# Loads of the side work of a hybrid trunk: three queues instead of one, two steps ahead, in finer steps

## The chip, the cores and the metric

The kernel runs on one core of a Trainium2 chip. The core has a matrix engine (TensorE, PE in the profile), a vector engine (VectorE, DVE), an activation engine (ScalarE, ACT), a general engine (GpSimd, POOL) and a synchronisation engine (SyncE, SP). Each takes its instructions in program order. SP, ACT and POOL can also issue transfers (DMAs) between the chip's main memory and the on-chip memory. The metric is the device time of one execution in microseconds (us), lower is better.

## The reference

One layer over 1024 tokens of width 1024, in float32. Four branches read one projection of the normalised input; their outputs are mapped back, merged by gates, projected, and a gated MLP with a short convolution follows. What matters here are three of the branches:

```python
# gMLP: v is normalised over 512 columns, then mixed over the 128 tokens of a block, per head
v = rms_norm(v, v_norm)
w = jnp.where(mask[None], w_s, 0)
sv = jnp.einsum('hts,bnshc->bnthc', w, v) + b_s.T[None, None, :, :, None]
return u * sv.reshape(bsz, seq, GMLP_WIDTH)

# RG-LRU: gates from small per-head products, then a scan over the tokens
r = sigmoid(einsum('bshi,hij->bshj', uh, w_a) + b_a)
log_a = -LRU_C * r * softplus(-lam)
h = scan(h * a + x_in) ; return h * gelu(y)

# gated linear attention (GLA), in chunks of 64 tokens
log_a = log_sigmoid(g_lr @ w_g2 + b_g) / GLA_TAU      # decays, summed up inside a chunk
# scaled queries and keys, then products inside chunks and a state across them
```

## The kernel before, in words

Every large product is made of three products of split operands: a tile is cast (ACT, line 122) and the rest is subtracted (DVE, line 123). On-chip tiles of 128 x 1024 come from one pool of 30 pages; raw weights have two buffers (`wr`).

The program runs in stages (times are those of the profiled execution):

- **gmlp**, 0 to 61 us: for each of 8 tiles of 128 tokens a norm (`hn`), a transpose and split (`hh` by ACT, `hl` by DVE), and the product for v. The normalised v (`vg`) is stored to main memory as `vgd`. The two `sm` instructions on POOL (lines 284 and 285) make a reciprocal root of a norm: one couple for `vg`, one for `hn`.
- **ranks**, to 117 us, then **columns**, 117 to 624 us: 24 *pairs* of column blocks. A pair is seven groups of 12 matmuls (`seven`, line 167), some 19 us of TensorE. Between the groups `work(s)` is called with s = 0 to 5. It applies the pair before's activation (`act`, ACT line 472), stores it (`fm<-za`, `fm<-zb`, POOL line 473), and from pair 4 on takes one step of the side work (`tick`).
- The **side work** is three generators that run one after another: `lru` (four heads), `spatial` (the gMLP mixing, four heads) and `factors` (the GLA's decays, queries and keys, for p = 0 and 1). A step ends at a `yield`. There are 95 ticks and 71 steps. Their inputs are pages in main memory that earlier pairs stored; `fetched_page` loads one, by POOL.
- **gla**, 624 to 718 us: an output gate (PE line 277), then `within` (lines 718 and 720) and `across` for each p and token tile. It reads six pages (`gl`) for each p, and four of `vd`.
- **mixing** and **latent** stages, attention, the merge and the MLP, to 1950 us. `load_o` loads a branch's output (`oraw`).

In columns and in the MLP the orders of ACT, DVE and SP are the order of the code (`manual_schedule`). Elsewhere, and always for PE and POOL, a scheduler orders the instructions when the kernel is built.

```python
def tick(self, n=1):
    for _ in range(n):
        while self.bg:
            try:
                next(self.bg[0])
                break
            except StopIteration:
                self.bg.popleft()
```

Of the kernel before, what the change touches and what calls it, by code (L numbers as in the profile page):

```python
# [17 lines left out]
P = 128  # L18
# [59 lines left out]
class Trunk:  # L78
# [262 lines left out]
    def gmlp(self):  # L341
# [41 lines left out]
        for i in range(NT):  # L383
            if i == 1:
                self.tc.no_sync_barrier()
            if i + 3 < NT:
                load(i + 3)
            if i + 2 < NT:
                norm(i + 2)
            if i == 6:  # L390
                wd = [self.pweights(a["wd"][0], 8, 264, 3)]
            v = self.page("vg")
            for n in range(2):
                ps = self.psum1()
                self.tm(ps[:, 0:256], self.hrows(i), wv[n])
                nc.scalar.activation(out=v[:, n * 256:(n + 1) * 256], in_=ps[:, 0:256], func=AF.Gelu_apprx_tanh)
                if n == 0 and i + 1 < NT:
                    next(step[i + 1], None)
            ss = self.small(1)
            nc.scalar.activation(out=v[:, 512:1024], in_=v[:, 0:512], func=AF.Square, accum_out=ss)  # L400
            r = self.rsqrt(ss, 512, 1)
            nc.vector.scalar_tensor_tensor(out=v[:, 0:512], in0=v[:, 0:512], scalar=r, in1=gv[:, 0:512], op0=ALU.mult, op1=ALU.mult)
            nc.gpsimd.dma_start(out=self.vgd[:, i * 512:(i + 1) * 512], in_=v[:, 0:512])
        wd.append(self.weights(a["wd"][1], 8, 264, 3))
# [54 lines left out]
    def columns(self, first):  # L459
# [28 lines left out]
        def work(s, prev, end):  # L488
# [25 lines left out]

    def fetched_page(self, src, name):
        t = self.page(name)
        self.nc.gpsimd.dma_start(out=t, in_=src)
        return t

    def spatial(self):  # L520
# [4 lines left out]
        w3 = ws[:, 0:512].rearrange("p (h t) -> p h t", h=4)  # L525
        vgd = self.vgd.rearrange("p (i c) -> p i c", i=NT)
        yield
        nc.vector.memset(w3[64:128, :, 0:64], 0.0)
        for h in range(4):
            v, u = self.page("vh"), self.fetched_page(self.fmo[h], "ug")  # L530
            v3 = v.rearrange("p (i c) -> p i c", i=NT)
            for i in (0, 4):
                nc.gpsimd.dma_start(out=v3[:, i:i + 4, :], in_=vgd[:, i:i + 4, h * P:(h + 1) * P])
            yield
# [10 lines left out]
    def lru(self):  # L545
# [20 lines left out]
        nc.vector.tensor_scalar(out=sm8, in0=sp4, scalar1=-2.0, scalar2=None, op0=ALU.mult)  # L566
        lraw = self.fetched_page(a["lw"], "lraw")
        yield
# [4 lines left out]
        for h in range(4):  # L573
            u = self.fetched_page(self.fmo[8 + h], "u")
# [7 lines left out]
            t, x = self.page("t"), self.page("xi")  # L582
            nc.scalar.activation(out=t, in_=ps, func=AF.Sigmoid, bias=prm[:, C_LBA + h:C_LBA + h + 1])
            ps = self.psum()
            self.fm(ps, [lw[4 + h]], [(uh, ul)])
            yield
            nc.scalar.activation(out=x, in_=ps, func=AF.Sigmoid, bias=prm[:, C_LBI + h:C_LBI + h + 1])
            u = self.fetched_page(self.fmo[8 + h], "u")
# [3 lines left out]
            nc.scalar.activation(out=t, in_=t, func=AF.Tanh, scale=sp4[:, h:h + 1])  # L592
            yield
            nc.scalar.activation(out=t, in_=t, func=AF.Sqrt)
            nc.vector.tensor_mul(out=x, in0=x, in1=u)
            yield
            nc.vector.scalar_tensor_tensor(out=x, in0=q, scalar=1.0, in1=x, op0=ALU.add, op1=ALU.mult)
            nc.vector.tensor_mul(out=x, in0=x, in1=t)
            y = self.fetched_page(self.fmo[4 + h], "yg")
            yield  # L600
            nc.vector.tensor_tensor_scan(out=t, data0=q, data1=x, initial=0.0, op0=ALU.mult, op1=ALU.add)
            yield
            nc.vector.tensor_mul(out=t, in0=t, in1=y)
            nc.gpsimd.dma_start(out=self.spill[1][h], in_=t)

    def factors(self):
# [5 lines left out]
        gd = self.page("gd")  # L612
        nc.gpsimd.dma_start(out=gd[:, 0:128], in_=self.gds[:, 0:128])
# [10 lines left out]
        nc.scalar.copy(out=gdt[0:16, :], in_=ps[0:16, :])  # L624
        yield
        for p in range(2):
            ps = self.psum()
# [3 lines left out]

            x, b = self.page("gx"), self.page("gb")
# [4 lines left out]
            nc.scalar.activation(out=b, in_=b, func=AF.Exp, scale=-1.0)  # L637
            nc.scalar.activation(out=b, in_=b, func=AF.Ln, bias=self.one)
            yield
            nc.vector.scalar_tensor_tensor(out=x, in0=x, scalar=0.0, in1=b, op0=ALU.min, op1=ALU.subtract)  # L640
            nc.gpsimd.dma_start(out=self.logs[p], in_=x)
            yield
        for p in range(2):
            x, b, keep = self.fetched_page(self.logs[p], "gx"), self.page("gb"), self.page("keep")
            nc.gpsimd.memset(keep, 1.0)
            nc.gpsimd.memset(c3(keep)[:, :, 0:1], 0.0)
            yield

            nc.vector.tensor_tensor_scan(out=b, data0=keep, data1=x, initial=0.0, op0=ALU.mult, op1=ALU.add)
            yield  # L650
            last, e2 = c3(b)[:, :, 63:64], self.page("e2")
            nc.vector.tensor_sub(out=c3(x), in0=last.to_broadcast([P, 16, 64]), in1=c3(b))
            nc.scalar.activation(out=dec[p].unsqueeze(2), in_=last, func=AF.Exp, scale=1.0 / 16)
            nc.scalar.activation(out=e2, in_=b, func=AF.Exp, scale=-1.0 / 16)
            k = self.fetched_page(self.fmo[14 + p], "qk")
            yield
            dv = dec[p].rearrange("p (b c) -> p b c", c=2)
            nc.vector.tensor_mul(out=self.dec2[p].unsqueeze(2), in0=dv[:, :, 0:1], in1=dv[:, :, 1:2])
            nc.scalar.activation(out=b, in_=b, func=AF.Exp, scale=1.0 / 16)
            nc.scalar.activation(out=x, in_=x, func=AF.Exp, scale=1.0 / 16)  # L660
            yield
            nc.vector.tensor_mul(out=e2, in0=e2, in1=k)
            nc.gpsimd.dma_start(out=self.glo[p][1], in_=e2)
            nc.vector.tensor_mul(out=x, in0=x, in1=k)
            nc.gpsimd.dma_start(out=self.glo[p][2], in_=x)
            q = self.fetched_page(self.fmo[12 + p], "qk")
# [13 lines left out]
            yield  # L680
            ps = self.psum()
            for i in range(NT):
                nc.tensor.transpose(ps[:, i * P:(i + 1) * P], ks2[:, i * P:(i + 1) * P], self.ident)
# [4 lines left out]
            kt = self.page("kt")  # L688
            nc.scalar.copy(out=kt, in_=ps)
            nc.gpsimd.dma_start(out=self.glo[p][5], in_=kt)  # L690

    def gla(self):
# [1000 lines left out]
```

## Time and profile before

| | us |
|---|---|
| median of 3 runs (1953.83 to 1956.97) | 1955.28 |
| the profiled execution, its own time | 1952.54 |
| its span, first to last instruction | 1950.8 |
| around the span (1952.54 - 1950.8) | 1.74 |
| TensorE busy | 1888.8 |
| VectorE, ScalarE, GpSimd busy | 1255.3, 866.9, 238.3 |

The granted clock of TensorE is 0.990 of its full speed over the span. The time is a median of a few executions and the profile is one of them.

### The profile page before, as it was taken

To read this page: it belongs to the slowest core of one execution; us is meant where nothing else is said; L and a number is where in the kernel's file an instruction comes from. 1 tells how busy PE (TensorE), PEld (TensorE's weight loads), DVE (VectorE), ACT (ScalarE), POOL (GpSimd) and SP (SyncE) were. 2 spreads that over 40 slices of the span, in tenths; PEclk is the share of its full clock that TensorE was granted. 3 is DMA by queue.
4 is the path that set the end of the run, shared out by engine and by line. 5 is a ranking of instruction groups with operands and counts; after the bars stand their busy time and mean duration, and the time that the engine had idled before them with its cause. 6 is when DMAs were issued, how large, how long until landed. Compare 5 with 4: busy or idle time off the path is not lost.

```text
span 1950.8 us, 25124 instructions
## 1 busy us (share of the span) xinstructions
PE 1888.8 (97%) x9768; PEld 1609.0 (82%) x9768; DVE 1255.3 (64%) x1752; ACT 866.9 (44%) x1329; POOL 238.3 (12%) x426
## 2 busy tenths in 40 slices
PE   7999999899999899999999999999999999999998
PEld 7988877678788898898788789978888888888887
DVE  4757667555754375717788972587777777774552
ACT  5433565436443132142677734355444444443331
POOL 2100100121202021011122300200000000000101
PEclk9999999899999899999999999999999999999999
DMA  6023344444635317316001343223233232686651
GB/s 241 24 87 130 130 162 161 168 159 153 235 137 195 143 66 267 101 57 220 30 23 32 138 160 132 97 86 108 107 109 117 106 120 101 207 318 214 256 192 44
DMA packets 84439, 269.75 MB, mean 138 GB/s; under 512 B 9584, under 2 KB 11264, under 8 KB 84320
## 3 DMA queue, kind: packets, MB, share of 16 engines
q1 hardware_dynamic: 53712, 157.90, 24.1%
q0 software_dynamic: 30464, 109.98, 14.8%
q8 instruction: 77, 1.26, 0.3%
q14 instruction: 42, 0.34, 0.1%
q10 hardware_dynamic: 144, 0.26, 0.0%
HBM read 187.30 MB, written 80.81 MB: 137 GB/s over the span
## 4 chain that ended last, share of the span: by engine, by line
PE 74%; issue 12%; DVE 6%; POOL 3%; ACT 3%; DMA 2%; POOLq 0%; SPq 0%; DVEq 0%; ACTq 0%
PE bk L167 22%; PE bk L1482 12%; PE ps L268 8%; PE ps L167 8%; PE p L277 8%; PE p L167 3%; PE ps L277 3%; PE ps L1024 2%; PE po L1075 2%; PE p L1209 2%; PE pp L1060 1%; POOL sm L285 1%; DMA oraw<-spill 1%; DVE wl L123 1%; POOL fm L473 1%
## 5 line engine op out<-in xcount | busy, mean ns | idle before, releaser
L122 ACT CAST wh<-t 128x1024 fp32r<-128x1024 f32 x85 | 89.5, 1053 | 295.2 <-PE bk L167 123.2
L167 PE MATMUL bk<-q,wh 128*128 128x512 f32 x704 | 217.0, 389 | 0.5 <-DVE q L123 0.5
L1482 PE MATMUL bk<-dh,g 128*128 128x512 f32 x704 | 217.0, 389 | 0.2 <-DVE q L1493 0.2
L123 DVE TENSOR_TENSOR wl<-wr,wh 128x1024 fp32r<-128x1024 f32 (+7 forms) x110 | 107.3, 977 | 128.4 <-ACT wh L122 127.5
L167 PE MATMUL ps<-S,wh 128*128 128x512 f32 x560 | 175.6, 394 | 3.6 <-ACT zb L216 3.6
L167 PEld LDWEIGHTS bk<-q,wh 128*128 128x128 f32 x704 | 132.1, 188 | 28.1 <-DVE q L123 0.8
L1482 PEld LDWEIGHTS bk<-dh,g 128*128 128x128 f32 x704 | 132.1, 188 | 28.0 <-DVE q L1493 0.6
L122 ACT CAST wh<-wr 128x1024 fp32r<-128x1024 f32 (+7 forms) x110 | 93.5, 852 | 130.9 <-PE ps L268 69.7
L268 PE MATMUL ps<-o,wh 128*128 128x512 f32 x512 | 140.6, 395 | 4.9 <-ACT o L122 2.8
L1482 PE MATMUL bk<-dl,g 128*128 128x512 f32 x352 | 136.9, 389 | 0.0
L167 PE MATMUL bk<-q,wl 128*128 128x512 f32 x352 | 136.9, 389 | 0.0
L167 PEld LDWEIGHTS ps<-S,wh 128*128 128x128 f32 x560 | 105.6, 190 | 27.3 <-ACT zb L216 5.3
L123 DVE TENSOR_TENSOR wl<-t,wh 128x1024 fp32r<-128x1024 f32 x85 | 103.8, 1222 | 34.2 <-ACT wh L122 34.1
L268 PEld LDWEIGHTS ps<-o,wh 128*128 128x128 f32 x512 | 95.5, 189 | 26.9 <-ACT o L122 3.7
L167 PE MATMUL ps<-S,wl 128*128 128x512 f32 x280 | 109.9, 393 | 0.0
L277 PE MATMUL p<-wl,hh 128*128 128x336 f32 (+2 forms) x320 | 94.8, 297 | 0.6 <-DVE wl L123 0.6
L277 PE MATMUL p<-wh,hh 128*128 128x336 f32 (+2 forms) x320 | 94.9, 298 | 0.0
L277 PE MATMUL p<-wh,hl 128*128 128x336 f32 (+2 forms) x320 | 94.8, 297 | 0.0
L167 PE MATMUL bk<-S,wh 128*128 128x512 f32 x304 | 93.5, 389 | 0.0
L123 DVE TENSOR_TENSOR dl<-dr,dh 128x1024 fp32r<-128x1024 f32 x44 | 53.8, 1222 | 43.4 <-ACT dh L122 36.4
L268 PE MATMUL ps<-o,wl 128*128 128x512 f32 x256 | 79.7, 392 | 0.8 <-DVE wl L123 0.8
L167 PEld LDWEIGHTS bk<-q,wl 128*128 128x128 f32 x352 | 66.1, 188 | 13.8
(447 smaller groups left out, 4617.3 us busy)
## 6 DMA issues: line engine op xcount, KB each, us to landing
wr<-in_wf SPq DMA_DIRECT2D x48, 512.0 KB, 4.3
wr<-in_up SPq DMA_DIRECT2D x44, 512.0 KB, 3.8
dr<-in_down SPq DMA_DIRECT2D x44, 512.0 KB, 5.3
g<-fm SPq DMA_DIRECT2D x32, 512.0 KB, 6.0
fm<-za POOLq DMA_DIRECT2D x22, 512.0 KB, 2.9
fm<-zb POOLq DMA_DIRECT2D x22, 512.0 KB, 2.9
gb<-fy POOLq DMA_DIRECT2D x22, 512.0 KB, 2.9
ga<-fy POOLq DMA_DIRECT2D x22, 512.0 KB, 2.9
```

Source lines behind the costliest of these rows:

```text
L122: self.nc.scalar.copy(out=hi, in_=src)
L123: self.nc.vector.tensor_sub(out=lo, in0=src, in1=hi.bitcast(F32))
L167: self.nc.tensor.matmul(ps, l[:, c], r, start=first and k == 0 and j == 0, stop=last and k == 3 and j == 2, skip_group_check=True)
L268: self.nc.tensor.matmul(ps[:, h * 512:(h + 1) * 512], lhs, rhs[:, h * 512:(h + 1) * 512], start=first and k == 0 and j == 0, stop=last and ...
L277: self.nc.tensor.matmul(ps, lhs, rhs, start=first and k == 0 and j == 0, stop=last and k == K - 1 and j == 2)
L285: nc.gpsimd.tensor_tensor(out=r, in0=t, in1=self.mhalf[:, 0:w], op=ALU.pow)
L473: nc.gpsimd.dma_start(out=self.fmo[idx], in_=z)
L1024: nc.tensor.matmul(ps[:, off + c0:off + c1], l[:, q0], r[:, c0:c1], start=jj == 0, stop=jj == 2)
L1060: nc.tensor.transpose(pp[:, at:at + P], probs[u][j][0][:, kb * P:(kb + 1) * P], self.ident)
L1075: nc.tensor.matmul(po[:, c], vs[2 * m + kk][:, head * P:(head + 1) * P], ptt[:, z * 512 + kk * 256:z * 512 + kk * 256 + c.stop - c.start], ...
L1209: self.nc.tensor.matmul(ps, l, x, start=k == 0 and j == 0, stop=k == K - 1 and j == 2)
L1482: nc.tensor.matmul(ps, l, r[:, halves[c]], start=first and n == 0 and j == 0, stop=last and n == len(gs) - 1 and j == 2)
```

## The change

1. gmlp's eight stores of `vg` to `vgd` are issued by SP instead of POOL.
2. `fetched_page` issues by SP unless it is given a queue; the side work gives it ACT's. So the loads of `lru`, `spatial` and `factors` (27 of them) are ACT's, and the GLA's pages, `vd` and the `oraw` loads are SP's.
3. The side work has finer steps: `lru` 40 instead of 35, `spatial` 10 instead of 9, `factors` 33 instead of 27. Loads stand about two steps ahead of their use. `spatial` loads head h + 1 while it works on head h, and a `vh` page comes by one DMA instead of two halves.
4. `factors` keeps the first decay page (p = 0) on chip; only that of p = 1 is stored and loaded again. Exp and Ln are taken for both p in succession.
5. In the last pair, at s = 5, four pages of p = 0 (1, 3, 4, 2) are loaded; `gla` then loads four of p = 1, then the rest.

```diff
-            nc.gpsimd.dma_start(out=self.vgd[:, i * 512:(i + 1) * 512], in_=v[:, 0:512])
+            nc.sync.dma_start(out=self.vgd[:, i * 512:(i + 1) * 512], in_=v[:, 0:512])
...
+            if end and s == 5:
+
+                self.gl = [{j: self.fetched_page(self.glo[0][j], "gl") for j in (1, 3, 4, 2)}, {}]
...
-    def fetched_page(self, src, name):
+    def fetched_page(self, src, name, queue=None):
         t = self.page(name)
-        self.nc.gpsimd.dma_start(out=t, in_=src)
+        (queue or self.nc.sync).dma_start(out=t, in_=src)
         return t
...
+        def fetch(h):
+            v = self.page("vh")
+            nc.scalar.dma_start(out=v.rearrange("p (i c) -> p i c", i=NT), in_=vgd[:, :, h * P:(h + 1) * P])
+            return v, self.fetched_page(self.fmo[h], "ug", nc.scalar)
+
+        nxt = fetch(0)
         yield
         nc.vector.memset(w3[64:128, :, 0:64], 0.0)
+        yield
         for h in range(4):
-            v, u = self.page("vh"), self.fetched_page(self.fmo[h], "ug")
-            v3 = v.rearrange("p (i c) -> p i c", i=NT)
-            for i in (0, 4):
-                nc.gpsimd.dma_start(out=v3[:, i:i + 4, :], in_=vgd[:, i:i + 4, h * P:(h + 1) * P])
+            v, u = nxt
+            if h < 3:
+                nxt = fetch(h + 1)
             yield
...
         for p in range(2):
-            x, b, keep = self.fetched_page(self.logs[p], "gx"), self.page("gb"), self.page("keep")
+            nc.scalar.activation(out=gb[p], in_=gb[p], func=AF.Exp, scale=-1.0)
+        yield
+        for p in range(2):
+            nc.scalar.activation(out=gb[p], in_=gb[p], func=AF.Ln, bias=self.one)
...
+        nc.gpsimd.dma_start(out=self.logs[1], in_=gx[1])
+        yield
+        x = gx[0]
+        for p in range(2):
+            if p:
+                x = self.fetched_page(self.logs[1], "gx", nc.scalar)
+            b, keep = self.page("gb"), self.page("keep")
             nc.gpsimd.memset(keep, 1.0)
             nc.gpsimd.memset(c3(keep)[:, :, 0:1], 0.0)
             yield
+            yield
...
+        for p, js in ((1, (1, 3, 4, 2)), (0, (5, 0)), (1, (5, 0))):
+            self.gl[p].update((j, self.fetched_page(self.glo[p][j], "gl")) for j in js)
         for p in range(2):
-            qs, ki, ks, qb0, qb1, kt = (self.fetched_page(t, "gl") for t in self.glo[p])
+            qs, ki, ks, qb0, qb1, kt = (self.gl[p][j] for j in range(6))
...
         if raw is None:
-            raw = self.page("oraw")
-            self.nc.gpsimd.dma_start(out=raw, in_=self.spill[k][h])
+            raw = self.fetched_page(self.spill[k][h], "oraw")
             yield
```

How the change moves instructions, at three places. Names carry the number of their buffer; `<-` has the target on its left.

**Place one, gmlp.** SP's order early in the program, before (`x` are the inputs of the norm, `wr` raw weights whose casts stand in ACT's order between those of `vg`):

```order
L349 DMA x_253<-in_x 128x1024
L349 DMA x_301<-in_x 128x1024
L349 DMA x_384<-in_x 128x1024
L131 DMA wr_943<-in_wd 128x792
L131 DMA wr_949<-in_wd 128x792
L349 DMA x_466<-in_x 128x1024
L131 DMA wr_955<-in_wd 128x528
```

and of the change:

```order
L349 DMA x_253<-in_x 128x1024
L349 DMA x_301<-in_x 128x1024
L403 DMA vgd<-vg_311 128x512
L349 DMA x_384<-in_x 128x1024
L131 DMA wr_943<-in_wd 128x792
L131 DMA wr_949<-in_wd 128x792
L349 DMA x_466<-in_x 128x1024
```

The first store of `vg` now stands ahead of three loads on SP, and is gone from POOL.

**Place two, the spatial mixing.** POOL's order before, in the pair in which `spatial` begins (`spill` is lru's last result, `fm` the pair's stores, `ws` the mixing weights and their bias, `ug` and `vh` the operands of one head):

```order
L604 DMA spill_3_90<-t_3126 128x1024
L473 DMA fm_121<-za_3089 128x1024
L473 DMA fm_122<-zb_3090 128x1024
L523 DMA ws_3276<-in_wst 128x512
L524 DMA ws_3276<-in_gmlp_b_s 128x512
L517 DMA ug_3300<-fm_99 128x1024
L533 DMA vh_3299<-vgd 128x4x128 x2
L517 DMA ug_3356<-fm_100 128x1024
L533 DMA vh_3355<-vgd 128x4x128 x2
```

and ACT's order of the change at the same place:

```order
L472 ACTIVATE za_3225<-za_3225 128x1024
L206 COPY za_3362<-p_430_3365 128x512
L472 ACTIVATE zb_3226<-zb_3226 128x1024
L533 DMA vh_3404<-vgd 128x8x128
L520 DMA ug_3406<-fm_99 128x1024
L216 COPY zb_3363<-ps_3364 128x512
L533 DMA vh_3442<-vgd 128x8x128
L520 DMA ug_3444<-fm_100 128x1024
L122 CAST wh_3446<-t_436_3408 128x1024
```

The operands of the heads have moved from POOL, behind `ws`, to ACT. The two loads of `ws` stay on POOL behind the same stores, and DVE's MEMSET of `ws`, which waits for the first of them, keeps its place between the pair's subtractions.

**Place three, the GLA's pages.** POOL's order before, at the end of the pairs (`fm_145` and `fm_146` are the last pair's stores; `gl_0_...` names a page's number, 155 to 160 are those of p = 0, 161 to 166 those of p = 1):

```order
L517 DMA gl_4966<-gl_5_160 128x1024
L517 DMA gl_4968<-gl_0_161 128x1024
L517 DMA gl_4970<-gl_1_162 128x1024
L473 DMA fm_145<-za_4825 128x1024
L473 DMA fm_146<-zb_4826 128x1024
L517 DMA gl_4972<-gl_2_163 128x1024
L517 DMA gl_4974<-gl_3_164 128x1024
L517 DMA gl_4976<-gl_4_165 128x1024
L517 DMA gl_4978<-gl_5_166 128x1024
```

and SP's order of the change (`wr<-in_wog` are the gate's weights, four loads of which the first two are issued early in the last pair, the third when a `wr` buffer comes free):

```order
L131 DMA wr_4901<-in_wog 128x1024
L520 DMA gl_4920<-gl_1_156 128x1024
L520 DMA gl_4922<-gl_3_158 128x1024
L520 DMA gl_4924<-gl_4_159 128x1024
L520 DMA gl_4926<-gl_2_157 128x1024
L131 DMA wr_4981<-in_wog 128x1024
L520 DMA gl_4957<-gl_1_162 128x1024
L520 DMA gl_4959<-gl_3_164 128x1024
L520 DMA gl_4961<-gl_4_165 128x1024
L520 DMA gl_4963<-gl_2_163 128x1024
```

The pages of p = 1 that `within` reads (1 to 4) no longer stand behind the last pair's stores; they stand behind the third load of the gate's weights.

## Rows read from the trace of the kernel before

**Rows 1.** The page: busy time, share of the span and instructions of each engine

```profile
PE 1888.8 (97%) x9768; PEld 1609.0 (82%) x9768; DVE 1255.3 (64%) x1752; ACT 866.9 (44%) x1329; POOL 238.3 (12%) x426
```

**Rows 2.** Waits of PE by cause: us in total, times, longest us

```profile
PE ps L537 <- DMA vh<-vgd: 12.0, 4, 7.0
...
PE ps L718 <- DMA gl<-gl: 7.2, 1, 7.2
PE ps L167 <- ACT zb L216: 3.6, 2, 2.9
PE ps L268 <- ACT o L122: 2.8, 2, 2.1
```

**Rows 3.** Stretches: us, busy of PE, PEld, DVE, ACT, POOL; clock, DMA share, GB/s

```profile
380.20:390.40 10.20, 5.02 (x19) 4.56 (x20) 2.70 (x4) 0.00 (x0) 2.07 (x3) 0.50 0.77 257
...
520.00:523.60 3.60, 2.94 (x7) 2.36 (x8) 2.83 (x3) 3.51 (x6) 0.50 (x1) 0.53 0.52 198
...
641.00:647.00 6.00, 5.71 (x29) 5.71 (x30) 1.53 (x5) 0.00 (x0) 0.53 (x1) 0.55 1.02 413
...
25.00:50.00 25.00, 23.65 (x199) 23.25 (x198) 13.52 (x15) 14.06 (x26) 8.29 (x18) 1.00 0.52 181
...
448.00:470.00 22.00, 22.00 (x94) 17.31 (x93) 13.33 (x18) 16.21 (x18) 2.67 (x5) 1.00 0.37 137
```

**Rows 4.** Spatial mixing in order of time: POOL (idle before, its cause)

```profile
373.42 0.56 POOL L523 DMA_DIRECT2D ws<-in_wst  x1
...
377.93 0.78 POOL L533 DMA_DIRECT2D vh<-vgd  x1 [2.80 <-issue]
```

**Rows 5.** The same for PE, DVE and ACT

```profile
383.32 2.04 PE L537 MATMUL ps<-ws,vh 128*128 128x128 f32 x8 [7.01 <-DMA vh<-vgd]
...
378.17 0.27 DVE L528 MEMSET ws<- 64x256 f32 x1 [4.26 <-DMA ws<-in_wst]
...
371.32 1.06 ACT L472 ACTIVATE zb<-zb 128x1024 f32<-128x1024 f32 x1
```

**Rows 6.** Transfers of 370 to 400 us: issues, KB each, median us to landing

```profile
vh<-vgd POOLq DMA_DIRECT2D x4, 256.0 KB, 3.5
...
ws<-in_gmlp_b_s POOLq DMA_DIRECT2D x1, 256.0 KB, 7.3
```

**Rows 7.** DVE in the factors, in order of time

```profile
509.56 2.29 DVE L649 TENSOR_TENSOR_SCAN gb<-keep,gx 128x1024 f32<-128x1024 f32 x1 [5.03 <-DMA gx<-log]
```

**Rows 8.** Around the start of gla in order of time: POOL, SP, PE

```profile
631.94 0.55 POOL L473 DMA_DIRECT2D fm<-za  x1 [9.01 <-ACT za L472]
...
633.49 2.42 POOL L517 DMA_DIRECT2D gl<-gl  x4
...
601.57 21.94 SPq L131 DMA_DIRECT2D wr<-in_wog  x4
...
641.29 1.65 PE L718 MATMUL ps<-gl,gl 128*128 128x128 f32 x6 [7.17 <-DMA gl<-gl]
```

**Rows 9.** The page: transfers of the whole kernel, as in rows 6

```profile
wr<-in_wf SPq DMA_DIRECT2D x48, 512.0 KB, 4.3
...
fm<-za POOLq DMA_DIRECT2D x22, 512.0 KB, 2.9
```

**Rows 10.** ACT at the start of mixing(3), in order of time

```profile
880.59 1.05 ACT L122 CAST o<-oraw 128x1024 fp32r<-128x1024 f32 x1 [3.18 <-DMA oraw<-spill]
```

**Rows 11.** gmlp, in order of time: POOL, ACT, PE

```profile
25.23 0.62 POOL L403 DMA_DIRECT2D vgd<-vg  x1 [1.08 <-DVE gq L943]
...
32.48 0.61 POOL L403 DMA_DIRECT2D vgd<-vg  x1 [1.08 <-DVE vg L402]
...
26.76 1.61 ACT L122 CAST wh<-wr 128x792 fp32r<-128x792 f32 x2
29.76 1.04 ACT L313 ACTIVATE hn<-x 128x1024 f32<-128x1024 f32 x1
...
37.13 0.39 PE L277 MATMUL p<-pwh,hl 128*128 128x256 f32 x1 [1.00 <-DVE hl L123]
```

More of the change, by code (lines that the diff above doesn't have):

```diff
@@ L566, in lru @@
         nc.vector.tensor_scalar(out=sm8, in0=sp4, scalar1=-2.0, scalar2=None, op0=ALU.mult)
-        lraw = self.fetched_page(a["lw"], "lraw")
+        lraw = self.fetched_page(a["lw"], "lraw", nc.scalar)
+        u = self.fetched_page(self.fmo[8], "u", nc.scalar)
+        yield
         yield
@@ L573, in lru @@
         for h in range(4):
-            u = self.fetched_page(self.fmo[8 + h], "u")
             yield
@@ L581, in lru @@
             yield
-            t, x = self.page("t"), self.page("xi")
+            t = self.page("t")
             nc.scalar.activation(out=t, in_=ps, func=AF.Sigmoid, bias=prm[:, C_LBA + h:C_LBA + h + 1])
@@ L585, in lru @@
             self.fm(ps, [lw[4 + h]], [(uh, ul)])
+            u = self.fetched_page(self.fmo[8 + h], "u", nc.scalar)
             yield
+            x = self.page("xi")
             nc.scalar.activation(out=x, in_=ps, func=AF.Sigmoid, bias=prm[:, C_LBI + h:C_LBI + h + 1])
-            u = self.fetched_page(self.fmo[8 + h], "u")
+            yield
             q = self.page("q")
@@ L592, in lru @@
             nc.scalar.activation(out=t, in_=t, func=AF.Tanh, scale=sp4[:, h:h + 1])
+            nc.vector.tensor_mul(out=x, in0=x, in1=u)
             yield
             nc.scalar.activation(out=t, in_=t, func=AF.Sqrt)
-            nc.vector.tensor_mul(out=x, in0=x, in1=u)
+            nc.vector.scalar_tensor_tensor(out=x, in0=q, scalar=1.0, in1=x, op0=ALU.add, op1=ALU.mult)
+            y = self.fetched_page(self.fmo[4 + h], "yg", nc.scalar)
             yield
-            nc.vector.scalar_tensor_tensor(out=x, in0=q, scalar=1.0, in1=x, op0=ALU.add, op1=ALU.mult)
             nc.vector.tensor_mul(out=x, in0=x, in1=t)
-            y = self.fetched_page(self.fmo[4 + h], "yg")
             yield
             nc.vector.tensor_tensor_scan(out=t, data0=q, data1=x, initial=0.0, op0=ALU.mult, op1=ALU.add)
+            if h < 3:
+                u = self.fetched_page(self.fmo[9 + h], "u", nc.scalar)
             yield
@@ L612, in factors @@
         gd = self.page("gd")
-        nc.gpsimd.dma_start(out=gd[:, 0:128], in_=self.gds[:, 0:128])
+        nc.scalar.dma_start(out=gd[:, 0:128], in_=self.gds[:, 0:128])
         w2, gdt = self.page("w2"), self.page("gdt")
@@ L625, in factors @@
         yield
+        gx, gb = [None] * 2, [None] * 2
         for p in range(2):
@@ L630, in factors @@
             yield
-            x, b = self.page("gx"), self.page("gb")
+            x, b = gx[p], gb[p] = self.page("gx"), self.page("gb")
             bg = prm[:, C_GBG + p:C_GBG + p + 1]
@@ L636, in factors @@
             yield
[L637 to L642, printed above, removed]
-        for p in range(2):
-            x, b, keep = self.fetched_page(self.logs[p], "gx"), self.page("gb"), self.page("keep")
+        for p in range(2):
+            nc.scalar.activation(out=gb[p], in_=gb[p], func=AF.Exp, scale=-1.0)
+        yield
+        for p in range(2):
+            nc.scalar.activation(out=gb[p], in_=gb[p], func=AF.Ln, bias=self.one)
+        yield
+        for p in range(2):
+            nc.vector.scalar_tensor_tensor(out=gx[p], in0=gx[p], scalar=0.0, in1=gb[p], op0=ALU.min, op1=ALU.subtract)
+        nc.gpsimd.dma_start(out=self.logs[1], in_=gx[1])
+        yield
+        x = gx[0]
+        for p in range(2):
+            if p:
+                x = self.fetched_page(self.logs[1], "gx", nc.scalar)
+            b, keep = self.page("gb"), self.page("keep")
             nc.gpsimd.memset(keep, 1.0)
@@ L647, in factors @@
             yield
+            yield
             nc.vector.tensor_tensor_scan(out=b, data0=keep, data1=x, initial=0.0, op0=ALU.mult, op1=ALU.add)
+            k = self.fetched_page(self.fmo[14 + p], "qk", nc.scalar)
             yield
@@ L652, in factors @@
             nc.vector.tensor_sub(out=c3(x), in0=last.to_broadcast([P, 16, 64]), in1=c3(b))
+            yield
             nc.scalar.activation(out=dec[p].unsqueeze(2), in_=last, func=AF.Exp, scale=1.0 / 16)
             nc.scalar.activation(out=e2, in_=b, func=AF.Exp, scale=-1.0 / 16)
-            k = self.fetched_page(self.fmo[14 + p], "qk")
             yield
@@ L658, in factors @@
             nc.vector.tensor_mul(out=self.dec2[p].unsqueeze(2), in0=dv[:, :, 0:1], in1=dv[:, :, 1:2])
+            nc.vector.tensor_mul(out=e2, in0=e2, in1=k)
+            nc.scalar.activation(out=x, in_=x, func=AF.Exp, scale=1.0 / 16)
+            nc.gpsimd.dma_start(out=self.glo[p][1], in_=e2)
+            q = self.fetched_page(self.fmo[12 + p], "qk", nc.scalar)
+            yield
             nc.scalar.activation(out=b, in_=b, func=AF.Exp, scale=1.0 / 16)
[L660 to L663, printed above, removed]
             nc.vector.tensor_mul(out=x, in0=x, in1=k)
             nc.gpsimd.dma_start(out=self.glo[p][2], in_=x)
-            q = self.fetched_page(self.fmo[12 + p], "qk")
             yield
@@ L671, in factors @@
             nc.vector.tensor_copy(out=s4[:, :, 1, :], in_=k4[:, :, 1, :])
+            yield
             nc.vector.tensor_mul(out=b, in0=b, in1=q)
             yield
+            ps = self.psum()
+            for i in range(NT):
+                nc.tensor.transpose(ps[:, i * P:(i + 1) * P], ks2[:, i * P:(i + 1) * P], self.ident)
             qb = [self.page("qb") for _ in range(2)]
@@ L680, in factors @@
             yield
-            ps = self.psum()
-            for i in range(NT):
-                nc.tensor.transpose(ps[:, i * P:(i + 1) * P], ks2[:, i * P:(i + 1) * P], self.ident)
+            kt = self.page("kt")
+            nc.scalar.copy(out=kt, in_=ps)
+            nc.gpsimd.dma_start(out=self.glo[p][5], in_=kt)
             q4 = b.rearrange("p (b c t) -> p b c t", c=2, t=64)
@@ L687, in factors @@
             yield
-            kt = self.page("kt")
-            nc.scalar.copy(out=kt, in_=ps)
-            nc.gpsimd.dma_start(out=self.glo[p][5], in_=kt)
     def gla(self):
```

## The prediction

> **What bounds the kernel now.** I read the page first: TensorE is busy for 1888.8 of 1950.8 us [rows 1], so only its 62 us of idleness, and the time in which it runs below full clock, are to be had. The view of its waits says for whom it stood: 12.0 us in four waits for the pages of the spatial mixing, 7.2 in one for the GLA's pages, 3.6 in two for ScalarE's copy `zb` (the longest 2.9), 2.8 in two for the casts of `oraw` [rows 2]. Then I took stretches behind these waits and looked at the granted clock. It stands at 0.50 to 0.55 behind the three long ones, which is the lower of its two levels (1.2 and 2.4 GHz), and at 1.00 in 25 to 50 us, where the engine had stood for only 1.00 us at a time [rows 3, 11]. A long wait therefore costs more than itself. I price the surplus as busy time x (1 - clock): 5.02 x 0.50 = 2.5, 2.94 x 0.47 = 1.4, and 5.71 x 0.45 = 2.6 us [rows 3]. Last, the orders by time show what each wait ends on.
>
> **Spatial mixing.** Before, POOL issues `ws`, then the heads' loads; the first `vh` half is issued at 377.93 after 2.80 of idleness that the profile lays to nothing else, and the product starts at 383.32 after 7.01 of standing [rows 4, 5]. The change issues `vh` by ScalarE behind the activation that ends at 372.4 [rows 5], and the later heads a step or more before their products. So 12.0 + 2.5 = 14.5 us go, less what is late next. Two things can be.
> First `ws`. It stays on POOL at its place, 373.42, and VectorE's MEMSET of it waits until 378.17 and ends at 378.44 [rows 4, 5]. In the change the first spatial product stands four matmuls later in TensorE's order than before (behind all 12 matmuls of the group S3, where it was behind 8). A matmul of the pairs takes 22.00/94 = 0.23 us [rows 3], and TensorE stopped at 383.32 - 7.01 = 376.3, so it comes there at 377.1 or so and stands 1.4 for the MEMSET. VectorE's own later work (three splits and an addition) is due about when TensorE needs it.
> Second the whole `vh` page. No row shows it in one transfer: it is 1024 pieces of 512 bytes where a half had 512. Halves land 3.5 us after issue, and the slowest load there took 7.3 [rows 6]; so the page lands between 375.9 and 379.7, and the wait is 0 to 2.6. Its issue costs ScalarE between 0.56 (POOL's for `ws`) and 3.6 (POOL's 0.78 with the idleness of 2.80 ahead) [rows 4]; I take the low end, for want of a cause of the 2.80 on ScalarE's queue. I take the page as landing no later than `ws` does, and keep 1.4 in all (0 to 4.3, which is the MEMSET's whole delay). Between a stand of 1.0 that left the clock alone and one of 2.9 that cost 1.4, I take half of that, 0.7. **Spatial: 14.5 - 2.1 = 12.4 gained.**
>
> **Factors.** VectorE's scan waits 5.03 for the page that has just been stored [rows 7]; all behind it is late, ScalarE's `zb` copy too, on which TensorE stands 2.9. For p = 0 the load is gone. For p = 1 it comes two steps ahead. **2.9 + 1.4 = 4.3 gained** (down to 0 if another step holds ScalarE there).
>
> **GLA's pages.** POOL holds the last four of the twelve behind the last pair's stores: 9.01 of waiting for ScalarE until 631.94, the pages from 633.49 [rows 8], and TensorE stands 7.2. In the change the four pages of p = 0 are issued after the second of the gate's weights, about 604. Those of p = 1 follow the third, which was issued about 622 when a `wr` buffer came free (the row of the four ends at 601.57 + 21.94 = 623.5) [rows 8]. At full load the DMAs move 413 GB/s [rows 3], so 0.5 MB takes 1.3 us. The weights land at 622 + 4.3 = 626.3 at the latest [rows 9], the four pages by 631.5. TensorE began to wait for p = 1 at 641.29 - 7.17 = 634.1 [rows 8], so 2.6 us are in hand. **7.2 + 2.6 = 9.8 gained.** Nine more loads follow (four `gl`, `vd`, the last weights) and end near 643 by the same 1.3; what reads them stands behind the products that 641 to 647 are full of.
> The stretch 641 to 647 has the DMA share at 1.02 [rows 3], so one may hold that transfers, not the issue, set the time. The Trainium skill (DMA: Bandwidth & Descriptors, section "Issuing engines are not separate DMA queues") says so in general: transfers issued by ScalarE, SyncE and GpSimd run on the same 16 DMA engines, and using several issuers only saves the time to initiate. Read that way, four issues of 2.42 us are the whole gain here, and the sum is 7.4 less. The row of 9.01 speaks against it: the pages waited for an activation, not for a DMA engine.
>
> **oraw.** ScalarE waits 3.18 for a page [rows 10]; of TensorE's 2.8 the shorter wait, 0.7, depends on it. SP isn't held by GpSimd's work. **0.7 gained** (0 to 2.8).
>
> **gmlp.** Here the change loses. The store of the first `vg` follows its data, at 25.23 [rows 11]. On SP the loads `x_384`, `wr_943` and `wr_949`, which waited for nothing of the kind, come behind it. With 0.56 for each issue [rows 4] the last leaves at 25.23 + 3 x 0.56 = 26.9, and lands 4.3 later, at 31.2 [rows 9]. ScalarE casts the second `wr` at 26.76 + 0.80 = 27.6 before [rows 11]; so all behind is 3.6 late, `hn` of the next tile too. But POOL is rid of its store. The square of `hn` ended at 29.76 + 1.04 = 30.8, yet its couple on POOL came behind the second store of `vg`, which waited for VectorE and ended at 32.48 + 0.61 = 33.1 [rows 11]. So 2.3 of the 3.6 come back, and TensorE stands 1.00 + 1.3 = 2.3 instead of 1.00 at 37. I take 1.3 and, as above, 0.7 for the clock: **2.0 lost** (0 to 3.6 + 1.4 = 5.0).
>
> **The rest.** ScalarE issues 27 loads at some 0.56 us: 15 us over 12 pairs, beside work that takes 16.21 of 22.00 even in a busy pair [rows 3], so they hide; without that cover they are 15 us. The finer steps add 12 ticks of the 24 unused ones and nothing to do. The smaller waits of TensorE in the pairs may change either way; I leave them.
>
> **Sum:** 12.4 + 4.3 + 9.8 + 0.7 - 2.0 = 25.2 us off the profiled execution's 1952.54, which gives 1927.3. The median stands 2.74 above that execution, so **1930.1**. About 0.2% (4 us) is what a measurement of this kernel can tell from no change.
>
> **The rivals.**
> *The heads still wait.* The whole `vh` page, or its place on an in-order engine, makes it land late: four products stand as long as the slowest load exceeds a half's, 7.3 - 3.5 = 3.8 for the first, less for the others, 7 to 10 us in all with the clock's share: 1937 to 1940. For it: the page's size and rows 6. Against: three of four loads are over ten microseconds ahead.
> *The transfers are the bound.* Then the stands only shift: the pages' issue of 2.42 and POOL's 2.80 are saved, gmlp's 2.0 lost: 3.2, so 1952. The rule of the Trainium skill cited above would have it so. For it: shares of 0.77 and 1.02. Against: the causes in rows 7 and 8 are late issues.
> *More is gained.* The gmlp store and the MEMSET cost nothing (+4.1), the longer `oraw` wait goes too (+2.1), and some small waits: 1923.
> *Slower.* ScalarE is in order. A load whose page was last read by a store waits for that store's landing, 2.9 us [rows 9], and the copies that empty TensorE's accumulators stand behind it. If each of the 27 loads cost TensorE 1.2, it would be 32 lost: 1930.1 + 32 = 1962. It decides from 25.2/27 = 0.93 a load. For it: TensorE has stood on just these copies. Against: ScalarE has some 6 us free in a pair of 22, and in the order only the last `ug` follows closely on the store it waits for.
>
> **How the numbers follow.** Likeliest 0.60 (its own range 1923 to 1939, by the bounds of `ws`, gmlp and `oraw`), heads late 0.13, more gained 0.10, transfers 0.07, slower 0.10. The range 1920 to 1946 leaves out the last two. Faster by over 0.2%: 0.60 + 0.13 + 0.10 = 0.83; same 0.07; slower 0.10.
>
> **What would show it.** Right: no wait for `vh` over 3 us, no half clock behind the GLA's first products, the first `gl` landing before 616, the scan without its 5 us; a longer wait for `hl` near 40 us; a MEMSET of `ws` still some 4 us late. Wrong: waits on `zb` or `za` copies that end behind a DMA on ScalarE, or TensorE waiting for `gl` behind the third weights.

## The result, and the profile after

The changed kernel takes **1935.53 us** (median of 4, 1934.66 to 1935.97) against 1954.93 beside it: a ratio of 0.9899, 95% interval 0.9882 to 0.9916. Predicted were 1930.1, 1920 to 1946. The profiled execution took 1935.97 with a span of 1934.2, so the spans differ by 16.6; before's profiled execution lay 2.4 below that median and the changed kernel's 0.4 above its own, which is the 2.8 between 16.6 and 19.4. Stages are compared by spans, whole kernels by medians.

TensorE's waits by cause show at once that the change did what it says and paid elsewhere (columns as in rows 2; the view's first line, 8.0 ahead of the first product as in the kernel before, and others are left out):

```profile
...
PE ps L268 <- DVE o L123: 5.9, 1, 5.9
PE ps L547 <- DVE ws L538: 3.6, 1, 3.6
PE p L277 <- ACT hh L122: 2.9, 2, 2.0
PE p L277 <- ACT vg L396: 2.7, 2, 1.9
...
PE p L277 <- DVE hl L123: 2.2, 2, 1.7
...
PE ps L268 <- ACT o L122: 1.8, 2, 1.5
```

The waits for `vh`, for `gl` and for `zb` of [rows 2] are gone. In their place stand one of 5.9 for a split of `oraw`, one of 3.6 for the MEMSET of `ws`, and new ones in gmlp. By stages, from TensorE's first instruction of each, this is the account of 16.6:

| stage | before | after | difference | predicted |
|---|---|---|---|---|
| gmlp and ranks, to the first pair | 116.6 | 121.7 | +5.1 | +2.0 |
| pairs, to the first `within` | 516.4 | 498.5 | -17.9 | -16.7 |
| gla and mixing(0), to the transposes behind it (729.8 before) | 96.7 | 86.8 | -9.9 | -9.8 |
| to the transposes of the latents | 164.3 | 170.1 | +5.8 | -0.7 |
| the rest of the span | 1056.7 | 1057.1 | +0.4 | 0 |

Each column is one profiled execution, and the same code doesn't take the same time in each. In the five traces with `vg`'s stores on SP the first pair begins at 118.3 to 123.4, in the eight with them on POOL at 115.5 to 116.8: the loss in gmlp is real, but lies between 1.5 and 7.9. The pairs of the kernel before took 519.5 in another build with the same code there (516.4 here), those of the changed kernel 498.4 and 500.1 in two others (498.5 here).

**The pairs.** Stretches of that stage (columns as in rows 3), first of the kernel before:

```profile
116.60:633.10 516.50, 497.96 (x2211) 405.41 (x2210) 317.11 (x406) 244.62 (x286) 72.24 (x127) 0.99 0.44 157
```

and of the changed kernel, with the stretch behind its stand at `ws`, one of gla, and the start of mixing(3):

```profile
121.70:620.20 498.50, 492.71 (x2211) 404.11 (x2210) 316.28 (x406) 242.18 (x283) 48.58 (x86) 1.00 0.45 161
402.00:406.00 4.00, 3.92 (x19) 3.74 (x20) 3.56 (x4) 0.00 (x0) 0.00 (x0) 0.62 1.04 329
625.00:650.00 25.00, 24.40 (x195) 23.72 (x194) 6.20 (x16) 4.98 (x11) 0.00 (x0) 1.00 0.41 152
851.00:871.00 20.00, 13.58 (x46) 10.36 (x47) 12.97 (x24) 5.27 (x10) 4.48 (x4) 0.83 0.31 111
70.00:76.00 6.00, 6.00 (x45) 6.00 (x45) 0.38 (x1) 1.15 (x3) 0.00 (x0) 0.84 0.11 44
```

TensorE is idle for 5.8 us of the pairs instead of 18.5, and busy for 492.7 instead of 498.0 with the same 2211 matmuls recorded: 12.7 came from waits and 5.3, by the granted clock (0.99 and 1.00), from the clock. One wait is new there. In order of time, POOL, then DVE and PE:

```profile
394.04 0.53 POOL L473 DMA_DIRECT2D fm<-zb  x1 [0.47 <-ACT zb L472]
394.76 0.56 POOL L526 DMA_DIRECT2D ws<-in_wst  x1 [0.19 <-issue]
```

```profile
401.71 0.27 DVE L538 MEMSET ws<- 64x256 f32 x1 [6.54 <-DMA ws<-in_wst]
```

```profile
402.08 2.28 PE L547 MATMUL ps<-ws,vh 128*128 128x128 f32 x13 [3.57 <-DVE ws L538]
```

`ws` left POOL at 394.76 and landed 6.8 later; then the MEMSET started, at 401.71. In the kernel before, behind the same three stores, it landed in 4.7 (columns as in rows 6; the changed kernel, then before):

```profile
ws<-in_wst POOLq DMA_DIRECT2D x1, 256.0 KB, 6.8
```

```profile
ws<-in_wst POOLq DMA_DIRECT2D x1, 256.0 KB, 4.7
```

**gmlp.** SP, ACT and PE of the changed kernel, in order of time:

```profile
24.74 0.33 SPq L403 DMA_DIRECT2D vgd<-vg  x1
25.11 0.43 SPq L349 DMA_DIRECT2D x<-in_x  x1
25.59 0.94 SPq L131 DMA_DIRECT2D wr<-in_wd  x2
...
63.05 0.33 SPq L403 DMA_DIRECT2D vgd<-vg  x1
63.42 0.43 SPq L335 DMA_DIRECT2D pwr<-in_wd  x1
```

```profile
30.89 1.81 ACT L122 CAST wh<-wr 128x792 fp32r<-128x792 f32 x2 [4.25 <-DMA wr<-in_wd]
...
66.68 0.63 ACT L122 CAST pwh<-pwr 128x528 fp32r<-128x528 f32 x1 [2.73 <-DMA pwr<-in_wd]
```

```profile
37.08 0.39 PE L277 MATMUL p<-pwh,hh 128*128 128x256 f32 x1 [0.91 <-ACT hh L122]
39.26 0.39 PE L277 MATMUL p<-pwh,hl 128*128 128x256 f32 x1 [1.67 <-DVE hl L123]
...
67.65 0.38 PE L277 MATMUL p<-pwh,hh 128*128 128x256 f32 x1 [1.89 <-ACT vg L396]
```

and ACT of the kernel before at the second place, where the cast waited for nothing:

```profile
62.44 0.63 ACT L122 CAST pwh<-pwr 128x528 fp32r<-128x528 f32 x1
```

The same thing happens twice: a load of weights leaves SP right behind a store that waited for its data, and ScalarE waits for it with `hh` and `vg` queued behind. The casts of `wr` start 4.1 later than in [rows 11].

**mixing(3).** DVE of the kernel before, in order of time (the 16 scalings of the latents stand between the last two lines):

```profile
874.47 1.23 DVE L123 TENSOR_TENSOR o<-oraw,o 128x1024 fp32r<-128x1024 f32 x1 [1.59 <-ACT o L122]
...
877.44 1.23 DVE L123 TENSOR_TENSOR o<-oraw,o 128x1024 fp32r<-128x1024 f32 x1 [0.26 <-ACT o L122]
...
884.68 2.36 DVE L123 TENSOR_TENSOR o<-oraw,o 128x1024 fp32r<-128x1024 f32 x2
```

and DVE, then PE, of the changed kernel:

```profile
851.42 1.23 DVE L123 TENSOR_TENSOR o<-oraw,o 128x1024 fp32r<-128x1024 f32 x1 [1.06 <-ACT o L122]
854.49 1.14 DVE L966 TENSOR_SCALAR ck<-ck,sm 128x256 f32<-128x256 f32 x4 [1.84 <-POOL sm L285]
856.65 1.41 DVE L967 TENSOR_SCALAR cq<-cq,sm 128x384 f32<-128x384 f32 x4 [1.02 <-POOL sm L285]
...
860.34 3.49 DVE L123 TENSOR_TENSOR o<-oraw,o 128x1024 fp32r<-128x1024 f32 x3
```

```profile
851.44 1.99 PE L268 MATMUL ps<-o,wh 128*128 128x512 f32 x6 [1.53 <-ACT o L122]
...
861.62 1.22 PE L268 MATMUL ps<-o,wh 128*128 128x512 f32 x2 [5.91 <-DVE o L123]
```

ScalarE has cast all four pages by 855.1. But in VectorE's order the 16 scalings of the latents now stand between the first subtraction and the second (before, between the second and the third), and they wait for POOL twice. TensorE stands for a subtraction that could have run at 852.7.

### The profile page after: what moved, and what is told of

It reads as the page before. It is cut to its first block, busy times and chain, and to the rows that moved or that the text cites. A ratio compares the mean times of both kernels' runs of the same rounds, so it can differ in the third digit from the quotient of the medians.

```text
span 1934.2 us, 25113 instructions
## 1 busy us (share of the span) xinstructions
PE 1883.1 (97%) x9768; PEld 1607.9 (83%) x9768; DVE 1255.3 (65%) x1752; ACT 863.7 (45%) x1326; POOL 199.0 (10%) x357
## 4 chain that ended last, share of the span: by engine, by line
PE 45%; DVE 3%; issue 1%; ACT 1%; POOL 1%; DMA 1%; POOLq 0%; DVEq 0%
PE bk L167 21%; PE bk L1510 12%; PE ps L277 3%; PE ps L268 2%; PE ps L1052 2%; PE po L1103 2%; PE p L1237 1%; PE pp L1088 1%; DVE ptt L123 0%; DVE sm L1057 0%; DMA oraw<-spill 0%; POOL sm L285 0%; DVE q L1295 0%; DVE qf L1033 0%; DMA wr<-in_up 0%
```

## The experiments

The theory at the outset: each part of the change acts in its own stage, the account above is the sum, and the three losses are separate. The rivals: the losses pass from one wait to the next, and what was gained came from the queue, or from the lead, alone. Ratios are to the kernel before on the same chip. Differences to the changed kernel are between medians of different rounds, in which the kernel before took 1953.57 to 1954.94; most ratios are known to 0.0015 or so, which is 3 us. So what an edit did is read from the stage that it touches, and the medians only have to agree with that.

**The stores of `vg` back on GpSimd.**

```diff
-            nc.sync.dma_start(out=self.vgd[:, i * 512:(i + 1) * 512], in_=v[:, 0:512])
+            nc.gpsimd.dma_start(out=self.vgd[:, i * 512:(i + 1) * 512], in_=v[:, 0:512])
```

> The changed kernel with only gmlp's eight stores of vg back on GpSimd. Theory: these stores on SyncE's queue hold the loads of the weights behind them twice (first the two wr and x loads, casts at 30.9 and 31.9 instead of 26.8 and 27.5; then the last pwr load at 63.4), and the pairs began at 121.69 instead of 116.64. Undone, the pairs begin at about 116.7, and the time falls by 5.0 from the changed kernel's 1935.5 to about 1930.5. Rival: GpSimd's couples of the norms were late because of these stores (they waited 1.1 for VectorE at every tile), so what comes back from the loads is lost there again: at most 1 gained, about 1934.5.

1930.03, ratio 0.9882 (0.9864 to 0.9899). The first pair begins at 116.4, 5.3 earlier. Of gmlp's waits after 30 us only before's remain, the longest this:

```profile
36.91 0.39 PE L277 MATMUL p<-pwh,hl 128*128 128x256 f32 x1 [0.99 <-DVE hl L123]
```

The theory holds; what GpSimd's relief gave was less than SP's load cost.

**The loads of `ws` by ScalarE, ahead of the heads' loads.**

```diff
-        nc.gpsimd.dma_start(out=ws[:, 0:512], in_=a["wst"])
-        nc.gpsimd.dma_start(out=ws[:, 512:1024], in_=a["gmlp_b_s"].partition_broadcast(P))
+        nc.scalar.dma_start(out=ws[:, 0:512], in_=a["wst"])
+        nc.scalar.dma_start(out=ws[:, 512:1024], in_=a["gmlp_b_s"].partition_broadcast(P))
```

> The changed kernel with the two loads of ws issued by ScalarE, ahead of the first head's loads, instead of by GpSimd behind three stores. Theory: TensorE's wait of 3.57 for the MEMSET of ws at 402 goes with the half clock behind it (3.92 busy at 0.62 in 402 to 406, 1.5): 5.1 less, about 1930.4, and the first spatial product waits for nothing over 0.5. Rival: the transfers crowd each other there (ws took 6.8 to land, beside four loads of 0.5 MB and three stores), so the wait passes to vh or to the split of the weights behind it: 1 less at most, about 1934.5.

1927.80, ratio 0.9869 (0.9853 to 0.9884): 7.7 less by the medians, 9.6 by the spans of the two traces. The pairs take 493.2 instead of 498.5, so 5.3 are this edit's, as expected; the rest lies in stages that the edit leaves alone, 1.0 in gmlp and 3.3 behind the gla stage, and is not explained by it. `ws` landed 2.8 after its issue instead of 6.8, and left some 5 earlier in the stage too, as it no longer stands behind three stores: the run doesn't separate the two. The first product of the spatial mixing starts without a wait:

```profile
397.47 1.24 PE L547 MATMUL ps<-ws,vh 128*128 128x128 f32 x9
```

**The next head's loads one step later** (against the reason that I gave for the slow `ws`).

```diff
             v, u = nxt
-            if h < 3:
-                nxt = fetch(h + 1)
             yield
+            if h < 3:
+                nxt = fetch(h + 1)
```

> The changed kernel with the loads of the next head (vh and ug) one step later, so that the second head's two pages no longer leave ScalarE just ahead of the loads of ws, which stay on GpSimd. Theory: ws took 6.8 to land because these two pages were on the way with it, where it took 4.7 in the kernel before; without them it lands some 2 earlier, and TensorE's wait for the MEMSET falls from 3.57 to about 1.5 with less half clock behind it: 3 less than the changed kernel, about 1932.5. Rival: ws is slow by the stores ahead of it and the first head's pages alone: the wait stays above 3, the time within 1 of 1935.5; a vh wait may come with a later head.

1935.14, ratio 0.9896 (0.9880 to 0.9913): no change from the changed kernel. TensorE still stands 3.0, the MEMSET 5.88:

```profile
402.70 0.27 DVE L538 MEMSET ws<- 64x256 f32 x1 [5.88 <-DMA ws<-in_wst]
```

So the theory falls: `ws` landed 6.1 after its issue, so the second head's pages took some 0.7 of the landing, not 2 (with them it landed in 6.9 and 7.5 in two other runs). The first head's pages and three stores are still ahead of `ws`. The stores alone don't make it slow: the kernel before has the same three ahead, and there it landed in 4.7. In the run with the queue alone (below), where the first head's pages leave ScalarE ahead of `ws` too, it landed in 6.1 as here. So the first head's pages are worth some 1.4, by single landings.

**VectorE's order in mixing(3) fixed**, the four subtractions first (`scale` holds the loop of the scalings, taken out of `latent`).

```diff
-            for h in range(4):
-                for _ in self.load_o(3, h, True, raws[h]):
-                    pass
+            with tc.manual_schedule(engines={mybir.EngineType.DVE}):
+                for h in range(4):
+                    for _ in self.load_o(3, h, True, raws[h]):
+                        pass
+                self.scale()
```

> The changed kernel with VectorE's order fixed at the start of the last mixing before the attention: the four subtractions of the oraw splits first, then the 16 scalings of the latents, which stood between the first and the second subtraction. Theory: TensorE's 5.91 wait there is VectorE's order and nothing of the transfers: it goes, with the half clock behind it (13.58 busy at 0.83 in 851 to 871, 2.3): 8 less, about 1927.5; the wait of 1.5 for the first cast stays. Rival one: what is late is the load or cast of oraw, so that nothing or under 1 comes back: 1935. Rival two: the scalings are wanted as early, and the wait moves to the transposes of the latents: 3 less, about 1932.5.

1928.27, ratio 0.9869 (0.9854 to 0.9884): 7.3 less. From the transposes of mixing(0) to the end it takes 8.3 less, and the granted clock is 1.00 over 840 to 860. The 5.91 wait is gone, and the scalings, now last, make nobody wait:

```profile
849.73 2.57 DVE L123 TENSOR_TENSOR o<-oraw,o 128x1024 fp32r<-128x1024 f32 x2 [1.06 <-ACT o L122]
852.53 2.36 DVE L123 TENSOR_TENSOR o<-oraw,o 128x1024 fp32r<-128x1024 f32 x2 [0.23 <-ACT o L122]
854.81 0.35 DVE L968 TENSOR_SCALAR ck<-ck,sm 128x256 f32<-128x256 f32 x1
```

**The kernel before with these four loads by SyncE**, and nothing else.

```diff
...
-                raws = [self.fetched_page(self.spill[3][h], "oraw") for h in range(4)]
+                raws = [self.fetched_page(self.spill[3][h], "oraw", self.nc.sync) for h in range(4)]
```

> The kernel before with one edit: the four oraw loads ahead of the last mixing before the attention are issued by SyncE. In this build VectorE's order there has one subtraction of oraw ahead of the 16 scalings, as the changed kernel has, where the kernel before has two. Theory: this edit alone brings the loss, since the schedule is made anew: TensorE stands 5.9 there instead of 2.1 and 0.7, the half clock lasts longer: 5 slower, about 1959.5. Rival: the pages come earlier than by GpSimd and that pays for the order: within 1.5 of before, about 1954.5.

1958.79, ratio 1.0024 (1.0014 to 1.0033), 5.1 slower. From the transposes of mixing(0) to those of the latents it takes 169.7 instead of 164.3. The one new line among TensorE's waits is that of the changed kernel:

```profile
PE ps L268 <- DVE o L123: 5.9, 1, 5.9
```

The edit that I had booked as a gain is a loss by itself, through an order on an engine that it doesn't name.

**The side work's part alone** (`vg`'s stores, the GLA's pages, `vd` and `oraw` as before).

```diff
-            if end and s == 5:
-                self.gl = [{j: self.fetched_page(self.glo[0][j], "gl") for j in (1, 3, 4, 2)}, {}]
...
-        (queue or self.nc.sync).dma_start(out=t, in_=src)
+        (queue or self.nc.gpsimd).dma_start(out=t, in_=src)
...
```

> The side work's part of the change alone (finer steps, its loads by ScalarE two steps ahead, the first decay page kept); vg's stores, the GLA's pages, vd and the oraw loads as before. Theory: the pairs lose the stands of 12.0 and 2.9 and their half clocks, and keep the 3.6 for the MEMSET of ws: the pairs' stage was 17.9 shorter in the changed kernel, so 17.9 less than before, about 1936.7. Rival: part of the 17.9 belongs to the shift of everything by the gmlp stage, and 13 or less is gained: 1941.5.

1932.03, ratio 0.9893 (0.9876 to 0.9909): 21.7 less than before. The pairs take 497.9, 18.5 less; the span is 22.3 shorter, so 3.8 lie in stages that the edit leaves alone, where single executions differ by nearly as much (see the stages above). The theory's size stands for the pairs; the surplus is not shown to be the edit's. `spatial` and `factors` were not measured apart.

**The queue without the lead**: the kernel before, its side work's loads by ScalarE at their old steps.

```diff
-            v, u = self.page("vh"), self.fetched_page(self.fmo[h], "ug")
+            v, u = self.page("vh"), self.fetched_page(self.fmo[h], "ug", nc.scalar)
...
-                nc.gpsimd.dma_start(out=v3[:, i:i + 4, :], in_=vgd[:, i:i + 4, h * P:(h + 1) * P])
+                nc.scalar.dma_start(out=v3[:, i:i + 4, :], in_=vgd[:, i:i + 4, h * P:(h + 1) * P])
...
```

> The kernel before with the side work's loads issued by ScalarE at their old steps (vh in halves): the queue without the lead. Theory: the idle stretches of GpSimd's queue go, but a load stands one step ahead of its use and the steps are some 3.8 apart, so of the 12.0 for vh some 4 stay, and of the factors' 2.9 some 2: 9 less, about 1945.5. Rival (another queue only saves the time to issue): some 3 less, 1951.5.

1939.14, ratio 0.9917 (0.9903 to 0.9932): 14.6 less, more than the theory's 9 and far more than the rival's 3; the pairs take 503.0 instead of 516.5. Of the waits for `vh` one of 0.99 is left, `zb`'s of 2.9 is gone, and `ws` takes their place:

```profile
PE ps L718 <- DMA gl<-gl: 6.4, 1, 6.4
PE ps L537 <- DVE ws L528: 4.0, 1, 4.0
```

**The lead without the queue**: the changed kernel, its side work's loads by GpSimd (a `vh` page in two halves).

```diff
-            return v, self.fetched_page(self.fmo[h], "ug", nc.scalar)
+            return v, self.fetched_page(self.fmo[h], "ug", nc.gpsimd)
...
```

> The changed kernel with all 27 loads of the side work issued by GpSimd again, at the same steps (a vh page in two halves): the lead without the queue. Theory: GpSimd's queue holds them behind stores that wait for ScalarE, and idles 2.8 to 4.8 ahead of each half of vh; waits for vh of 3 to 8 in all come back: about 1941. Rival (the lead alone counts, the queue only saves time to issue): no wait for vh over 1, the same time as the changed kernel, 1935.5 within 2.

1939.13, ratio 0.9912 (0.9895 to 0.9928): 3.6 slower than the changed kernel by the medians. The two ratios' intervals overlap; in the traces the pairs take 502.2 instead of 498.5, so the 3.7 lie where the edit is. `vh` is waited for again, and POOL idles before its halves as in [rows 4]:

```profile
PE ps L549 <- DMA vh<-vgd: 6.6, 2, 3.5
```

```profile
397.94 0.77 POOL L535 DMA_DIRECT2D vh<-vgd  x1 [2.10 <-issue]
402.39 0.77 POOL L535 DMA_DIRECT2D vh<-vgd  x1 [3.68 <-issue]
```

The rival of the lead alone falls. The halves come with the queue here; by ScalarE, in the run before this one, the halves were waited for only 0.99 in all. But the two remedies overlap: the queue alone gave 14.6, the lead with the old queue is 3.6 short of both, and both gave 21.7.

**The GLA's part alone, by SyncE, and the same order by GpSimd.**

```diff
+            if end and s == 5:
+                self.gl = [{j: self.fetched_page(self.glo[0][j], "gl", self.nc.sync) for j in (1, 3, 4, 2)}, {}]
...
```

> The kernel before with the GLA's part of the change alone: four gl pages in the last pair, the rest in the new order, all of them and vd by SyncE. Theory: TensorE's 7.2 wait goes with the half clock behind it (2.6), and nothing else moves: 9.8 less than before's 1954.6, about 1944.8. Rival (the transfers are the bound there): the wait shrinks by the issue time alone, 2.4 less, about 1952.

With `nc.gpsimd` in the same places:

> As the run with the GLA's part alone, but issued by GpSimd, in the same new order: the pages that TensorE needs first now stand ahead of the last pair's two stores on GpSimd's queue too. Theory: it is the place in the queue that counts, so the same 9.8 are gained; in this build VectorE's order at the start of the last mixing before the attention has all four subtractions of oraw ahead of the scalings (before had two), which gives some 2 more: about 1943. Rival (SyncE's queue is what helps): pages still late by some of the 7.2, 4 or less gained, about 1951.

1945.31, ratio 0.9949 (0.9934 to 0.9964), and 1944.07, ratio 0.9944 (0.9929 to 0.9959): 9.3 and 10.5 less. From the first `within` to the transposes of mixing(0) both take 86.8, as the changed kernel does (96.7 before). By GpSimd the eight pages leave ahead of the last pair's stores, which wait 10.74 for ScalarE as before:

```profile
622.48 0.53 POOL L519 DMA_DIRECT2D gl<-gl  x1 [0.72 <-DMA gl<-gl]
633.74 0.55 POOL L473 DMA_DIRECT2D fm<-za  x1 [10.74 <-ACT za L472]
```

The place in the queue counts here, not whose queue it is. GpSimd's build also has a better order in mixing(3), so its 1.2 of advantage says nothing of the queues.

**The three mends together**: `vg`'s stores by GpSimd, `ws` by ScalarE, VectorE's order fixed.

> The changed kernel with three mends together: vg's stores by GpSimd, the loads of ws by ScalarE ahead of the heads' loads, VectorE's order fixed with the four subtractions of oraw first. Theory: the three losses lie in different stages and add up: 5.5, 7.7 and 7.3 less than 1935.5, about 1915. Rival: part of each passes to the next wait behind it, some 12 in all, about 1923.

1916.87 (1914.49 to 1917.92), ratio 0.9803 (0.9788 to 0.9818): 18.7 less than the changed kernel, where the three apart gave 5.5, 7.7 and 7.3, or 20.5: nearly all, and not the rival's 12. It is faster than both. TensorE's waits are led by the first load and by stages that the change doesn't touch:

```profile
PE ps L319 <- DVE hn L315: 7.9, 1, 7.9
PE ps L1317 <- DVE q L123: 2.4, 1, 2.4
PE p L277 <- DVE hl L123: 2.2, 4, 1.0
```

## Why the prediction was right, and where its steps failed

**Spatial mixing and factors** (12.4 + 4.3): right in mechanism, 17.9 for 16.7; the scan no longer waits for its page either. Two sizes were off and cancelled, which is luck. The term for `ws` was 1.4 and measured 3.57: I kept the landing time of before, 4.7, and the earlier loads of the heads were on the way as well, so that it took 6.8; moving `ws` ahead of them and of the stores recovered 5.3. (Two readings were off, without weight: 376.3 + 4 x 0.23 is 377.2, so the sum gives a stand of 1.2; and 7.3 is the largest of the rows' medians, while the first `ug` took 7.9.) The price of the clock was 3.9 less 0.7; the pairs' busy time fell by 5.3. Busy time x (1 - clock) over one stretch behind each long wait leaves out what the shorter stands cost: in [rows 2] four stands make the 12.0. This reason is argued, not measured.

**GLA** (9.8): right, 9.9 in the stage and 9.3 alone. The rule of the Trainium skill (DMA: Bandwidth & Descriptors, section "Issuing engines are not separate DMA queues") agrees with the two runs of the GLA's part, 9.9 in the stage by SyncE and by GpSimd alike. Read as the prediction read it, it would misprice the side work: there the queue alone was worth 14.6. GpSimd's queue idled 2.75 to 4.83 us ahead of each half of `vh` in the kernel before, and a load there stood behind the pair's stores. No run shows how the 14.6 divide between the two.

**oraw** (0.7 gained): this step failed, with its sign. The pages did come early. I took VectorE's order to stay, though the scheduler makes it anew at that place; the changed order could have been read before the run. TensorE stood 5.9 there: 5.8 lost in the stage, and 5.4 in that stage when the loads alone were moved.

**gmlp** (2.0 lost): the mechanism was right at its first place, the size short there (TensorE stood 3.4 at three places between 30 and 40 us, where it had stood 1.0 at one; I had 2.3), and a second place was missed: the seventh store ahead of the last `pwr` load, 1.89 and half clock behind it. Undone, 5.3 came back, just over the upper end of my bound (5.0).

**The rest**: the 27 loads did hide, as I said. The rival *slower* found nothing: no wait on `zb` is left. It isn't empty, though: with `ws` on ScalarE too, one load took 2.20 to issue and ScalarE stood 2.28 before the cast behind it, without a wait of TensorE. *The heads still wait* came true only with the loads on GpSimd.

**The sum.** By spans, 25.2 were forecast and 16.6 came: 8.6 short, mostly `oraw` (6.5) and gmlp (3.1), less 1.2 that the pairs gave on top. The median misses by only 5.4, because the offset of 2.74 between profile and median did not hold for the changed kernel, whose profiled execution was 0.44 above its median. That is chance. The time lies in the range with one term's sign wrong and another's size too small.

## What to carry to other kernels

A load that waits behind a store is late by the store's data, on SP's queue (gmlp) as on POOL's (the GLA's pages): write down each queue's neighbours after the move, not only before. Where a scheduler makes an engine's order, compare that order at every place whose inputs now come at another time, also on engines that the edit doesn't name. And loads that are moved earlier can slow one that is issued beside them (`ws` landed in 6.8 instead of 4.7); move the one that is needed first, first.

## What the runs showed of the hardware

In these traces ScalarE issues a transfer ahead of activations that stand before it in its order, so its order doesn't tell when a load of its leaves. In the order of the change `vh` stands behind the activation of `zb`; ACT of the changed kernel, in order of time (ACTq is its issue):

```profile
389.97 0.59 ACTq L533 DMA_DIRECT2D vh<-vgd  x1
...
392.58 1.06 ACT L472 ACTIVATE zb<-zb 128x1024 f32<-128x1024 f32 x1
```

It left 2.6 us before that activation began. In the run with the queue alone the first `vh` left at 366.89, and the activation of `zb` began at 369.15. This fits that the queue alone gave more than I expected, since a load on ScalarE isn't as late as its place says; how much of the surplus it is was not measured.

TensorE's clock fell to its lower level behind a single stand of 1.89 us (0.84 over 70 to 76) and one of 3.57 (0.62), and didn't in the changed kernel behind three of 0.81, 0.91 and 1.67 within 7 us. The length of a stand doesn't decide it. With the same gmlp code, the run with `ws` on ScalarE had stands of 0.96, 0.83 and 1.73 at these three places and the lower level behind them; the run with the next head's loads later stood 2.23 at the fourth place and kept its clock. Two stretches (columns as in rows 3), of the one, then of the other:

```profile
40.00:44.00 4.00, 4.00 (x23) 4.00 (x22) 0.95 (x1) 0.41 (x2) 0.00 (x0) 0.58 0.68 240
```

```profile
71.00:77.00 6.00, 6.00 (x51) 6.00 (x52) 1.04 (x2) 1.27 (x5) 0.74 (x2) 1.00 0.11 44
```

So the price of such a stand can't be told from one trace. The run with VectorE's order fixed, in which no stretch of gmlp behind these four places fell, has the earliest first pair of the five, at 118.3.
